# Merge and first feed-forward group in written order, with loads and casts ahead

## The chip, the cores and the metric

The kernel runs on one core of one Trainium2 chip. A core has four engines that compute and that this text names by the profile's letters too: TensorE (PE, matmuls; PEld is its weight load), VectorE (DVE), ScalarE (ACT) and GpSimd (POOL). A fifth, SyncE (SP), issues nearly all transfers between the chip's main memory (HBM) and the core's working memory (SBUF); ScalarE issues a few. Matmul results land in eight accumulation banks (PSUM). Each engine works through its own list of instructions in order, and waits at an instruction until the semaphores that it needs are up. The metric is the device time of one execution in microseconds; lower is better.

## The reference

One layer of a transformer-like block over 2048 latent tokens and 256 context tokens of width 1024, all in float32:

```python
mod = silu(c) @ w_mod + b_mod                 # sh1, sc1, g1, sh2, sc2, g2
h = modulate(x, norm1_g, sh1, sc1)
k, v, q, u, vg, ga, gb = split(h @ w_in)      # one projection
attn = attention(rope(q), [ctx keys, keys], [ctx values, values])
gm = gelu(u) * (gm_ws @ rmsnorm(gelu(vg)) + gm_bs)
y = sigmoid(ga) * (attn @ w_br_attn) + sigmoid(gb) * (gm @ w_br_gm)
x1 = x + g1 * (y @ w_out)                     # the "merge"
h2 = modulate(x1, norm2_g, sh2, sc2)
out = x1 + g2 * (relu(h2 @ w_ff1) ** 2 @ w_ff2)   # the feed-forward part
```

## The kernel before

Every float32 operand is split into a high part (a cast, on ScalarE) and the remainder (a subtraction, on VectorE or GpSimd), and a product is three matmuls: high x high, high x low, low x high (`mm3`, L183 to L185; `product`, L1502 to L1504). `split` (L150, L154) makes the two parts. The large products of the feed-forward part use a scheme of seven block products instead of eight (numbered 0 to 6), whose operands are sums and differences of blocks.

The stages, in order: input projection and gMLP (to about 730 us), attention (to 1436), the merge, and then for each of two blocks of 1024 tokens the first products (`ff1`) and the second products (`ff2`).

*The merge* goes over 4 blocks b of 512 tokens. For each, 8 branch steps m compute 128 columns of the merged rows y: 12 matmuls with the gMLP inputs and 12 with the attention inputs, each followed by a product with a gate on VectorE (L1268); the two are added (L1271) and y is split. Then the output projection: for four groups tt of 128 tokens and two halves n, 24 matmuls over the 8 parts of y, a product with the gate g1 (L1313), the residual addition (L1314), a store of x1 and a sum of squares on ScalarE (L1320). Around this, other work is woven in as Python generators that are advanced step by step: `load_w_out` (the output weights, in block 0), `br_inputs` (the inputs of the next block), `mod_part` (the modulation vectors sh2 and sc2: sixteen loads of `w_mod` each, multiplied and added up on VectorE, summed over the partitions by small matmuls) and, in the last block, `h_first` (reads x1 back, scales it (L1356), transposes it on TensorE (L189, evacuated at L1369) and makes the operands of the first products) and `w1_ops` (weights of the first products: L1450, L1451, L1456 to L1472).

*The feed-forward part.* `ff1` runs 16 groups of 256 hidden columns, each with the seven products (`ff1_group`), and stores its operands for the second half to HBM (`ao_d`). `ff2` reads them back with the second weights (`w2o_d`) in 56 chunks, casts each (L1607, L1608) and multiplies; a generator `side` runs beside it: the gate g2 (`last_gate`) and the operands of the next block (`h_ops`).

*What sets the order.* A scheduler orders the instructions of each engine by its own estimate of when they are ready, earlier-written first. `order()` at the end can forbid that: instructions in a range listed in `pins` keep the written order on every engine; those in `fixed` keep it on TensorE and VectorE alone. Before the change the attention is `fixed` and each `ff2` is pinned; the merge and `ff1` are neither. Working memory is handed out in rings: a tag with n slots (`POOLS`, L55 on) gives a new tile the slot of an old one, and its first write waits until the old one's last reader is done. Tags that matter here: `bw` (14, branch weights), `gt` (6, gates), `raw` (3) and `gx` (2) for input rows, `md` (5, modulation), `wo` (18, output weights), `xt` (3, residual rows), `f8` (2, x1 blocks and raw first weights), `b4` (12, first weights and second-product chunks). Pools are opened and closed by stage, so that the first tiles of a new pool wait for the last readers of the old ones.

Of the kernel before, what the change touches and what calls it, by code (L numbers as in the profile page):

```python
# [70 lines left out]
class Kern:  # L71
# [280 lines left out]
    def mod_part(self, alloc, names):  # L352
        nc, I = self.nc, self.I
        for what in names:
            at = 2 * D + ("g1", "sh2", "sc2", "g2").index(what) * D
            for n in range(2):
                lo, sl = at + n * TB, slice(n * TB, (n + 1) * TB)
                acc = alloc()
                for k in range(KC):
                    w = alloc()  # L360
                    nc.sync.dma_start(w, I["w_mod"][0, k * P : (k + 1) * P, lo : lo + TB])
                    s = self.silu[:, k, 0:1]
                    if k == 0:
                        nc.vector.tensor_scalar(
                            out=acc, in0=w, scalar1=s, scalar2=None, op0=ALU.mult
                        )
                    else:
                        nc.vector.scalar_tensor_tensor(
                            out=acc, in0=w, scalar=s, in1=acc, op0=ALU.mult, op1=ALU.add
                        )  # L370
                    if k % 2:
                        yield
                yield
                if what in ("g1", "g2"):
                    dst = (self.g1b if what == "g1" else self.g2b)[:, sl]
                    nc.sync.dma_start(
                        dst, I["b_mod"][:, lo : lo + TB].partition_broadcast(P)[:, 0, :]
                    )
                    ps = self.bank([TB])
                    nc.tensor.matmul(ps, self.ones, acc, start=True, stop=True)  # L380
                    nc.vector.tensor_tensor(out=dst, in0=ps, in1=dst, op=ALU.add)
                    if what == "g1":
                        nc.vector.tensor_scalar(
                            out=dst, in0=dst, scalar1=0.5, scalar2=None, op0=ALU.mult
                        )
                else:
                    ks = slice(n * HK, (n + 1) * HK)
                    bc = self.small([HK])
                    nc.sync.dma_start(
                        bc, I["b_mod"][:, lo : lo + TB].rearrange("o (k p) -> p (o k)", p=P)  # L390
                    )
                    ps = self.bank([HK])
                    for k in range(HK):
                        nc.tensor.matmul(
                            ps[:, k : k + 1], acc[:, k * P : (k + 1) * P],
                            self.ones[:, :1], start=True, stop=True,
                        )
                    dst = (self.S2 if what == "sh2" else self.G2)[:, ks]
                    nc.vector.tensor_tensor(out=dst, in0=ps, in1=bc, op=ALU.add)
                    if what == "sc2":  # L400
                        n2 = self.small([HK])
                        nc.sync.dma_start(
                            n2,
                            I["norm2_g"].rearrange("o (k p) -> p (o k)", p=P)[:, ks],
                        )
                        nc.vector.scalar_tensor_tensor(
                            out=dst, in0=dst, scalar=1.0, in1=n2, op0=ALU.add, op1=ALU.mult,
                        )
                yield

    def last_gate(self):
        nc, I = self.nc, self.I

        def fetch(n, k):
            lo = 5 * D + n * TB
            w = self.sb("f2", [TB])
            nc.sync.dma_start(w, I["w_mod"][0, k * P : (k + 1) * P, lo : lo + TB])
            return w

        steps = [(n, k) for n in range(2) for k in range(0, KC, 2)]  # L420
        nc.sync.dma_start(
            self.g2b, I["b_mod"][:, 5 * D : 6 * D].partition_broadcast(P)[:, 0, :]
        )
        ahead = [fetch(0, k) for k in range(2)]
        yield
        accs = []
        for i, (n, k0) in enumerate(steps):
            ws = ahead
            if i + 1 < len(steps):
                ahead = [fetch(steps[i + 1][0], steps[i + 1][1] + j) for j in range(2)]  # L430
            if k0 == 0:
                accs.append(self.sb("f2", [TB]))
            for k, w in zip((k0, k0 + 1), ws):
                s, acc = self.silu[:, k, 0:1], accs[n]
# [4 lines left out]
                else:  # L439
                    nc.vector.scalar_tensor_tensor(  # L440
                        out=acc, in0=w, scalar=s, in1=acc, op0=ALU.mult, op1=ALU.add
                    )
            yield
        for n in range(2):
            dst = self.g2b[:, n * TB : (n + 1) * TB]
            ps = self.bank([TB])
# [1728 lines left out]
```

## Time and profile before

| | |
|---|---|
| time, median of 3 executions (range) | 3094.04 us (3090.9 to 3099.88) |
| time of the profiled execution | 3104.55 us |
| span in its profile | 3102.5 us |
| mean granted TensorE clock | 0.983 |
| TensorE busy | 2994.0 us (97%) |
| VectorE, ScalarE, GpSimd busy | 2074.6, 1459.5, 689.0 us |
| moved by transfers | 534.32 MB |

The profile comes from one execution, recorded by the hardware. A row of a timeline gives start, duration, engine, line and operation, what is written from what (names of tiles without numbers), and in brackets how long the engine had been idle before it and which instruction of which engine released it. A row of a table by groups gives the number of instructions, their busy time and mean duration in ns, then the idle time before them. A row of a table by windows gives for each engine the busy time and in brackets the number of instructions, then the granted TensorE clock as a share of full speed, the busy share of the transfer engines and what they moved. Matmuls overlap in the array, so one row of 0.39 us may start 0.23 us after the one before.

### The profile page before, as it was taken

To read this page: it belongs to the slowest core of one execution; us is meant where nothing else is said; L and a number is where in the kernel's file an instruction comes from. 1 tells how busy PE (TensorE), PEld (TensorE's weight loads), DVE (VectorE), ACT (ScalarE), POOL (GpSimd) and SP (SyncE) were. 2 spreads that over 40 slices of the span, in tenths; PEclk is the share of its full clock that TensorE was granted. 3 is DMA by queue.
4 is the path that set the end of the run, shared out by engine and by line. 5 is a ranking of instruction groups with operands and counts; after the bars stand their busy time and mean duration, and the time that the engine had idled before them with its cause. 6 is when DMAs were issued, how large, how long until landed. Compare 5 with 4: busy or idle time off the path is not lost.

```text
span 3102.5 us, 38027 instructions
## 1 busy us (share of the span) xinstructions
PE 2994.0 (97%) x13501; PEld 2262.9 (73%) x13501; DVE 2074.6 (67%) x2990; ACT 1459.5 (47%) x2352; POOL 689.0 (22%) x506
## 2 busy tenths in 40 slices
PE   6999999979999999999989999999999999999999
PEld 4877788766555555556867878887878888878887
DVE  4767578875887667777654478775676666654555
ACT  5645765654555454554222155443454344444432
POOL 0000000001988888885134300000000000000000
PEclk9999999999999999999999999999999999999999
DMA  8676666644110000005865448887776544438554
GB/s 296 202 259 212 226 197 198 205 145 129 35 35 28 14 15 8 11 15 185 265 203 164 137 156 316 310 301 278 256 234 220 191 153 153 154 139 285 204 200 153
DMA packets 386478, 534.32 MB, mean 172 GB/s; under 512 B 32928, under 2 KB 204112, under 8 KB 386288
## 3 DMA queue, kind: packets, MB, share of 16 engines
q1 hardware_dynamic: 376512, 515.89, 49.7%
q10 hardware_dynamic: 9776, 16.01, 1.4%
q8 instruction: 106, 1.74, 0.2%
q14 instruction: 84, 0.69, 0.1%
HBM read 367.69 MB, written 164.10 MB: 171 GB/s over the span
## 4 chain that ended last, share of the span: by engine, by line
PE 83%; DMA 6%; DVE 5%; ACT 2%; issue 2%; POOL 1%; SPq 0%; ACTq 0%; DVEq 0%; POOLq 0%
PE b L1502 14%; PE b L1503 14%; PE b L1504 14%; PE b L2067 8%; PE b L2034 5%; PE b L2053 4%; PE b L183 3%; PE b L185 3%; PE b L184 3%; PE a L1502 3%; PE b L1999 3%; PE a L1503 3%; PE a L1504 3%; PE b L189 2%; DMA bw<-in_w_br_gm 1%
## 5 line engine op out<-in xcount | busy, mean ns | idle before, releaser
L2010 DVE TENSOR_REDUCE ts<-b 128x1 f32<-128x512 f32 x512 | 314.7, 681 | 141.6 <-PE b L1999 141.5
L2083 POOL TENSOR_TENSOR ac<-ac,p 128x512 f32<-128x512 f32 x216 | 301.5, 1428 | 67.7 <-ACT p L2057 67.0
L1608 DVE TENSOR_TENSOR b<-b,b 128x1024 fp32r<-128x1024 f32 x168 | 198.6, 1221 | 145.0 <-ACT b L1607 144.6
L1607 ACT CAST b<-b 128x1024 fp32r<-128x1024 f32 x168 | 168.7, 1051 | 240.0 <-PE b L1503 222.0
L2057 ACT ACTIVATE p<-b 128x512 f32<-128x512 f32 x384 | 199.8, 616 | 166.5 <-PE b L2053 156.6
L1502 PE MATMUL b<-b,b 128*128 128x512 f32 x672 | 263.9, 393 | 8.6 <-ACT b L1607 7.9
L1503 PE MATMUL b<-b,b 128*128 128x512 f32 x672 | 263.1, 391 | 2.4 <-DVE b L1608 2.4
L1504 PE MATMUL b<-b,b 128*128 128x512 f32 x672 | 262.6, 391 | 0.0
L2083 POOL TENSOR_TENSOR ac<-ac,t 128x512 f32<-128x512 f32 x152 | 217.6, 1457 | 0.0
L2034 PE MATMUL b<-h,h 128*128 128x512 f32 x576 | 200.9, 419 | 0.9 <-DVE ts L2010 0.4
L2053 PE MATMUL b<-h,h 128*128 128x512 f32 x576 | 180.3, 394 | 0.0
L2067 PE MATMUL b<-p,h 128*64 128x512 f32 x768 | 175.3, 598 | 0.0
L1503 PE MATMUL b<-hb,b 128*128 128x512 f32 x448 | 174.6, 390 | 0.0
L1956 POOL MEMSET t<- 128x512 f32 x16 | 8.4, 525 | 701.9 <-DMA tb_d<-t 679.8
L1502 PE MATMUL b<-hb,b 128*128 128x512 f32 x416 | 162.0, 389 | 0.0
L1504 PE MATMUL b<-hb,b 128*128 128x512 f32 x416 | 161.7, 389 | 0.0
L1512 DVE TENSOR_TENSOR f<-f,b 128x512 f32<-128x512 f32 x160 | 109.2, 682 | 77.7 <-issue 46.1
L1502 PEld LDWEIGHTS b<-b,b 128*128 128x128 f32 x672 | 126.9, 189 | 36.6 <-ACT b L1607 9.2
L2034 PEld LDWEIGHTS b<-h,h 128*128 128x128 f32 x576 | 106.7, 190 | 58.4 <-DVE ts L2010 19.4
L1503 PEld LDWEIGHTS b<-b,b 128*128 128x128 f32 x672 | 126.8, 189 | 30.0 <-DVE b L1608 3.7
L1504 PEld LDWEIGHTS b<-b,b 128*128 128x128 f32 x672 | 126.8, 189 | 26.5
L1502 PE MATMUL a<-f,h 128*128 128x384 f32 (+1 forms) x320 | 118.7, 376 | 12.8 <-ACT f L647 6.3
(409 smaller groups left out, 7435.0 us busy)
## 6 DMA issues: line engine op xcount, KB each, us to landing
ao_d<-f SPq DMA_DIRECT2D x224, 256.0 KB
f<-in_w_ff SPq DMA_DIRECT2D x48, 1024.0 KB
b<-ao_d SPq DMA_DIRECT2D x84, 512.0 KB
b<-w2o_d SPq DMA_DIRECT2D x84, 512.0 KB
w2o_d<-f SPq DMA_DIRECT2D x112, 256.0 KB
f<-in_w_in SPq DMA_DIRECT2D x44, 512.0 KB
f<-x_d SPq DMA_DIRECT2D x64, 256.0 KB
hb<-ao_d SPq DMA_DIRECT2D x56, 256.0 KB
```

Source lines behind the costliest of these rows:

```text
L1502: mm(ps, wh, hh, start=start and k == 0, stop=False, skip_group_check=True)
L1503: mm(ps, wh, hl, start=False, stop=False, skip_group_check=True)
L1504: mm(ps, wl, hh, start=False, stop=k == len(w) - 1, skip_group_check=True)
L1512: nc.vector.tensor_tensor(out=out, in0=in0, in1=in1, op=op)
L1607: nc.scalar.copy(h, f32(l))
L1608: nc.vector.tensor_tensor(out=l, in0=f32(l), in1=f32(h), op=ALU.subtract)
L2010: nc.vector.tensor_reduce(out=self.mx[:, t, h, c : c + 1], in_=ps[h], axis=AX.X, op=ALU.max)
L2034: self.nc.tensor.matmul(self.pts[j][h], k.KA[c][self.kv][:, ks], self.qa[h], start=True, stop=False, skip_group_check=True,)
L2053: self.nc.tensor.matmul(s, k.KB[c][self.kv][:, ks], self.qb[h], start=False, stop=True, skip_group_check=True,)
L2057: self.nc.scalar.activation(pt[h], s, AF.Exp)
L2067: nc.tensor.matmul(self.o[h * HD : (h + 1) * HD, :], k.V[c][:, i, self.kv * HD : (self.kv + 1) * HD], pt[h], start=j == 0, stop=j == NKT - 1,)
L2083: nc.gpsimd.tensor_tensor(out=self.acc[e][:, h], in0=old[:, h], in1=pt[h], op=ALU.add)
```

## The change

- The whole merge, from its first load to the last residual store, is a pinned range: every engine keeps the written order.
- Branch step n issues the loads of raw weights and gates of step n+2 and casts the weights of n+1. Before, it loaded and cast those of n+2 together. Remainders of weights go to GpSimd from the third step on (before: in blocks 1 to 3); the remainder of y goes from GpSimd to VectorE.
- `load_w_out`, `br_inputs`, the residual rows and `mod_part` fetch one step ahead. The broadcast row sums of `br_inputs` use the tag `gx`. The store of x1 and its square come after the next group's first products. `next(side)` and `next(mod)` come before the two VectorE operations of the projection instead of after them.
- `mod_part` loads its bias at the start of a part instead of at its end, and does g2 as well, in place of `last_gate`.
- `h_first` scales a block one step before it is transposed, and makes the sums one step after. The merge advances it by 1 + 7 steps, and by 2 more after the pinned range. The casts of the very first weights take a slot of `f8` in place of two of `b4`.
- In the very first group of `ff1`, product 5 comes after product 1.
- The first block's second products load three chunks ahead instead of two, and the first two chunks are loaded before the last group of first products.

The core of the diff:

```diff
     def load_w_out(self):
         ...
-        for k in range(KC):
+        ahead = fetch(0)
+        yield
+        for k in range(KC):
+            st = ahead
+            if k + 1 < KC:
+                ahead = fetch(k + 1)
             h, l = self.sb("wo", [D], F32R), self.sb("wo", [D], F32R)
             self.split(st, h, l, lo_eng="dve")
     def merge(self, first, start, last, ops, w1):
         ...
+        begin = self.here()
         steps = [(b, m) for b in range(NB) for m in range(KC)]
         ...
+        def load(n, tag="gt"):
+            raws[n] = self.br_raw(steps[n][1])
+            gts[n] = self.gate_in(*steps[n], tag)
+
+        def cast(n, lo_eng):
+            ws[n] = self.br_weights(raws.pop(n), lo_eng)
...
+        load(0, "gx")
+        load(1)
+        cast(0, "dve")
+        next(w_out)
         for b in range(NB):
             y = []
             for m in range(KC):
-                fetch("pool" if b else "dve")
-                ws, gt = q.pop(0)
+                n = b * KC + m
+                if n + 2 < len(steps):
+                    load(n + 2)
+                if n + 1 < len(steps):
+                    cast(n + 1, "pool" if n > 1 else "dve")
+                w, gt = ws.pop(n), gts.pop(n)
...
-                self.split(gt["a"], yh, yl)
+                self.split(gt["a"], yh, yl, lo_eng="dve")
...
+            next(side)
+            xt, done = x_row(b, 0), None
             for tt in range(TT):
-                xt = self.sb("xt", [D])
-                nc.sync.dma_start(xt, self.x_block(b)[tok, :])
+                after = x_row(b, tt + 1) if tt + 1 < TT else None
...
                     outer(n, range(head if tt == 0 else 0, KC))
+                    if n == 0 and done:
+                        stored(*done)
+                        done = None
+                    if b + 1 < NB or (tt, n) < (TT - 1, 1):
+                        next(side, None)
+                    next(mod, None)
                     part = self.sb("jk", [512])
                     nc.vector.tensor_tensor(out=part, in0=ps, in1=self.g1b[:, cs], op=ALU.mult)
                     nc.vector.tensor_tensor(out=xt[:, cs], in0=xt[:, cs], in1=part, op=ALU.add)
-                    next(side, None)
-                    next(mod, None)
-                nc.sync.dma_start(self.x1_d[b][tok, :], xt)
...
+                done, xt = (b, tt, xt), after
+            stored(*done)
...
+        self.pins.append(range(begin, self.here()))
+        for _ in range(2):
+            next(side)
     def h_first(self, ops, w1):
+        x, raw = self.x1_load(0, 0), None
+        yield
+        for kk in range(HK):
+            self.x1_scaled(x, r)
+            if kk:
+                sums(kk - 1, raw)
+            yield
+            raw = self.x1_turned(x, kk)
+            if kk + 1 < HK:
+                x = self.x1_load(0, kk + 1)
+            else:
+                next(w1)
+            yield
+        sums(HK - 1, raw)
+        next(w1)
+        yield
     def w1_ops(self, g, out, first=False):
-        hr, lr = self.sb("b4", [KC, P], F32R), self.sb("b4", [KC, P], F32R)
+        if g == 0 and first:
+            both = self.sb("f8", [2, KC, P], F32R)
+            hr, lr = both[:, 0], both[:, 1]
...
     def ff1_group(self, blk, g, w, h):
-        self.product(pb, w[5], h[5], True)
-        u2 = self.sb("f2", [TB])
-        tt(u2, u3, pb, add)
-        yield
+        if g or blk:
+            u2 = fifth()
+            yield
         self.product(pa, w[1], h[1], False)
...
+        if not g and not blk:
+            u2 = fifth()
+            yield
     def ff1(self, blk, h, extra, w=None, late=()):
-                self.ready = [self.ff2_cast(self.ff2_load(blk, 0, 0))]
+                raws = [self.ff2_load(blk, 0, c) for c in range(2)]
+                self.ready = [self.ff2_cast(raws.pop(0))], raws
     def ff2(self, blk, side):
-        ahead = 4 if blk else 2
+        ahead = 4 if blk else 3
...
-        ready = self.ready
-        raws = [load(n) for n in range(1, ahead)]
+        ready, raws = self.ready
+        raws += [load(n) for n in range(2, ahead)]
     def ffn(self, h, w, w1, late):
-        next(late)
-        next(late)
+        next(late)
...
-        side = chain(self.last_gate(), self.h_ops(1, h))
+        side = chain(
+            self.mod_part(lambda: self.sb("f2", [TB]), ("g2",), True), self.h_ops(1, h)
+        )
```

252 lines of the change are left out of this document (123 added, 129 removed).

## The prediction

> **What bounds the kernel now.** I read the page first, the busy time of the engines.
>
> ```profile
> span 3102.5 us, 38027 instructions
> PE 2994.0 (97%) x13501; PEld 2262.9 (73%) x13501; DVE 2074.6 (67%) x2990; ACT 1459.5 (47%) x2352; POOL 689.0 (22%) x506
> ```
>
> TensorE is busy 97% of the span, so an edit that removes no matmuls can win only where TensorE idles, or runs at a lowered clock after idling. The changed code runs from 1436.7 us (first branch product of the merge) to about 2520 us (end of the first block's second products). The waits of TensorE told me where to cut that stretch; this view gives busy time and counts of each window.
>
> ```profile
> core 0: us, PE busy (x) PEld busy (x) DVE busy (x) ACT busy (x) POOL busy (x), PEclk, DMA share, GB/s
> 1436.70:1553.00 116.30, 116.22 (x497) 93.06 (x498) 80.56 (x111) 37.58 (x60) 23.36 (x16) 0.99 0.84 269
> 1553.00:1605.00 52.00, 42.37 (x162) 31.47 (x161) 34.58 (x38) 13.68 (x24) 26.35 (x19) 0.90 0.67 216
> 1678.00:1705.00 27.00, 23.13 (x88) 17.89 (x87) 12.94 (x18) 8.60 (x15) 8.01 (x7) 0.87 0.61 199
> 1705.00:1776.00 71.00, 71.00 (x314) 57.94 (x313) 27.63 (x39) 13.94 (x25) 22.99 (x17) 1.00 0.39 126
> 1828.00:1846.00 18.00, 12.59 (x34) 8.83 (x35) 16.42 (x23) 12.11 (x19) 0.00 (x0) 0.72 0.45 149
> 1846.00:2150.00 304.00, 304.00 (x1334) 249.95 (x1333) 236.98 (x325) 144.60 (x212) 0.00 (x0) 1.00 0.83 293
> 2150.00:2170.00 20.00, 12.38 (x41) 9.32 (x40) 8.03 (x8) 6.18 (x6) 0.00 (x0) 0.74 0.99 346
> ```
>
> The counts tell more than the busy time. Undisturbed, the merge does 314 matmuls in 71 us: 4.42 per us, 0.226 us each. Against that rate the second window lacks 52 x 4.42 - 162 = 68 matmuls (15.3 us), the third 31 (7.1 us), the one at 1828 lacks 46 (10.3 us), the one at 2150 lacks 47 (10.7 us). These figures hold idle time and lowered clock together. So 43 us, 1.4%, is there to be won; the rows of 1.00 clock are full.
>
> What makes the first hole is seen in the timelines of ScalarE, VectorE and TensorE (start, duration, instruction, idle time before it and its releaser).
>
> ```profile
> 1583.01 0.62 ACT L150 CAST bw<-bw 128x512 fp32r<-128x512 f32 x1 [4.73 <-DMA bw<-in_w_br_gm]
> 1585.34 0.62 ACT L150 CAST bw<-bw 128x512 fp32r<-128x512 f32 x1 [1.71 <-POOL bw L154]
> 1585.87 1.13 ACT L150 CAST in<-raw 128x512 fp32r<-128x512 f32 x2
> 1586.90 0.62 ACT L150 CAST y<-gt 128x512 fp32r<-128x512 f32 x1
> ...
> 1583.50 0.69 DVE L1271 TENSOR_TENSOR gt<-gt,gt 128x512 f32<-128x512 f32 x1
> ...
> 1587.58 0.80 PE L183 MATMUL b<-wo,y 128*128 128x512 f32 x1 [5.30 <-ACT y L150]
> ```
>
> The merged rows y that the output projection needs are added up by 1584.2 (L1271), but ScalarE casts them only at 1586.90: they stand in its queue behind weights for later steps, which wait for their load and for GpSimd. TensorE idles 5.30 us for sums that were ready after 2 of them.
>
> The hole at 2150 is another kind:
>
> ```profile
> 2149.34 0.32 SPq L1560 DMA_DIRECT2D ao_d<-f  x1
> 2150.09 0.37 SPq L1595 DMA_DIRECT2D b<-ao_d  x1
> ...
> 2155.43 1.04 ACT L1607 CAST b<-b 128x1024 fp32r<-128x1024 f32 x1 [6.84 <-DMA b<-ao_d]
> ...
> 2157.86 0.80 PE L1502 MATMUL b<-b,b 128*128 128x512 f32 x1 [7.15 <-ACT b L1607]
> ```
>
> Chunk 1 of the second products is loaded only after the group's last stores, takes 5.3 us to its cast, and TensorE has nothing for 7.15 us.
>
> **The change, part by part.** *Merge in program order.* No matmul, cast or gate load goes away; their order does. Within step n, ScalarE now casts the weights of n+1 and then y of n. The load of those weights was issued two steps ahead; residual rows, `w_out`, the next block's inputs and the modulation weights are issued one step ahead. A step is 24 matmuls, 5.4 us, so two steps are 10.9 us, against the 5.3 us that the load above took at the fullest DMA (share 0.99). Newly queued: SyncE, in order, holds the gate loads of n+2 until y of n-1 is split, which frees their slots, and the raw weights of n+3 stand behind them; they are still issued about 10 us before their cast. The groups of the two middle blocks (1553 to 1776 us) give the loop that is left:
>
> ```profile
> L154 POOL TENSOR_TENSOR bw<-bw,bw 128x512 fp32r<-128x512 f32 x38 | 50.7, 1348 | 131.3 <-ACT bw L150 131.3
> L154 POOL TENSOR_TENSOR y<-gt,y 128x512 fp32r<-128x512 f32 x22 | 32.0, 1457 | 9.9 <-ACT y L150 9.9
> ...
> L150 ACT CAST bw<-bw 128x512 fp32r<-128x512 f32 x38 | 22.4, 619 | 86.6 <-DMA bw<-in_w_br_gm 68.8 <-POOL bw L154 10.8 <-PE b L185 6.2
> ...
> L1268 DVE SCALAR_TENSOR_TENSOR gt<-gt,b 128x512 f32<-128x512 f32 x43 | 29.0, 683 | 46.8 <-PE b L185 46.8
> L1271 DVE TENSOR_TENSOR gt<-gt,gt 128x512 f32<-128x512 f32 x21 | 19.4, 923 | 0.6
> L154 DVE TENSOR_TENSOR in<-raw,in 128x512 fp32r<-128x512 f32 x16 | 15.2, 953 | 19.9 <-ACT in L150 19.9
> ```
>
> From the end of step n: gate product 0.68, addition 0.92, y on ScalarE 0.62, the cast of the weights of n+2 0.62, GpSimd's remainder 1.35: 4.2 us; in block 0 the cast of a `w_out` row comes between (128x1024, 1.04 like L1607 above): 5.2 us. That remainder is first read by the third matmul of step n+2, 5.4 + 0.5 = 5.9 us later. So the loop closes with 1.7 us to spare, in block 0 with 0.7. GpSimd's load falls from 2 x 1.35 + 1.46 = 4.2 us a step to 2.7; VectorE's rises by the 0.95 of y's remainder to 2 x 0.68 + 0.92 + 0.95 = 3.2 us, in block 0 by a wider `w_out` remainder more. Both stay below 5.4. In the output projection VectorE has, per 24 matmuls, one input row (a product 0.69 as the single L1271 above, a remainder 0.95), two modulation rows (taken as 0.92 each) and two additions (0.69 each): 4.9 us. That is tight too, but it holds TensorE up only if the block's last input is late, and this one has 12 matmuls of gMLP products (2.7 us) as cover; with the cover gone I would expect 2 us at each of three block starts. I take both holes as gone, -22.4 us, and put 2.5 us back for these tight places, nearer to none than to the bound, as the loop has slack in every block (bounds 0 and +9, which is about one us in each step of block 0).
>
> The subtraction that moves from GpSimd to VectorE now runs beside GpSimd's remainders. The Trainium skill, "SBUF — State Buffer", in its part on the port that both engines share, says that a VectorE instruction with two SBUF inputs is shut out for the whole of a GpSimd instruction that reads SBUF. The groups agree in direction: 0.92 and 0.95 with two SBUF inputs, 0.68 with one in PSUM. At worst, by that rule, y would come 1.35 us later, which uses up most of the slack.
>
> *End of the merge, first group.* The hole at 1828, ScalarE and then TensorE:
>
> ```profile
> 1829.37 1.06 ACT L1320 ACTIVATE jk<-xt 128x1024 bf16<-128x1024 f32 x1 [5.59 <-DVE xt L1314]
> 1830.33 0.19 ACT L1320 ACTIVATION_READ_ACCUMULATOR jk<-xt 128x1 f32 x1
> 1830.42 1.03 ACT L1450 CAST b<-f 128x1024 fp32r<-128x1024 f32 x1
> 1831.36 0.77 ACT L1369 ACTIVATE f<-b,S,G 128x512 f32<-128x512 f32 x1
> ...
> 1831.50 0.80 PE L1502 MATMUL b<-in,b 128*128 128x512 f32 x1 [3.62 <-ACT b L1450]
> ...
> 1839.85 0.50 PE L1504 MATMUL b<-in,b 128*128 128x512 f32 x1 [1.68 <-DVE b L1466]
> ```
>
> The last 16 transposes move from before the last projection to after it, and product 5, which waited 1.68 us, comes after product 1 and so gets 12 matmuls, 2.7 us, more. Against that, the new buffer for the first weights (L1450) is free only when these transposes are done, and the four activations out of them (0.77 each), the square (1.06) and one cast (0.62) can stand ahead of it on ScalarE: 4.8 us, of which some 0.3 to 1.3 us lie before the transposes' end. That puts the first product 3.5 to 4.5 us after the transposes, against 3.62 us of wait before. VectorE was busy 16.42 of 18 us and has the same work. I take 0 (bounds -5, half the hole, and +6).
>
> *Second products.* Chunk 1 is now loaded before the last group of first products, so TensorE goes on at 2150.7 for 24 matmuls, to 2156.1. Chunk 2 is then the first that is loaded at 2150.1; it lands as chunk 1 did, and its first matmul can start at 2157.9: 1.8 us of idle, 1 us more for its remainder on VectorE, and an estimated 2 us of lowered clock after that. 10.7 becomes 4.8, so -5.9 us (bounds -10.7 and 0, the latter if the extra 1 MB finds no free slot in the last group). In the steady state the twelve slots are as full before as after. On the clock, the window at 1678, whose granted mean is 0.87, lost 27 x 0.13 = 3.5 us in that way. The Trainium skill, "TensorE: Matmul & The Clock Gate", Part 1, says that the clock halves after an idle window of about 3.4 us; by that rule a wait of 2.8 us would cost no clock and the sum would be 2 us lower.
>
> *The rest.* Gate g2 takes 13 instead of 10 of 56 slots, bias loads come earlier, the attention's last input loads one step ahead. None of them ends a wait of TensorE in the rows above: 0. If the cover of the g2 slots went, its first use in step 15 of 56 would be late by at most those 3 slots.
>
> Sum: -22.4 + 2.5 + 0 - 5.9 = -25.8 us. The profiled execution took 3104.55 us, 10.5 above the median of 3094.04; taken off the median, 3068.
>
> **Rivals.** *A, slower: the loop of a branch step is longer than a step.* VectorE's split of y and GpSimd's remainders delay each other, and ScalarE, in program order, casts the next weights behind y. From 1.7 us of delay on TensorE waits in every step; at 2.6 us it loses 0.9 us in each of 29 steps and the gain is gone; at 3.2 us it loses 1.5 x 29 = 43 us: 3068 + 43 = 3111. For it: 953 against 683 ns. Against: GpSimd's load falls by a third. *B: the holes stay by half*, because the loads are late and not the casts' order: SyncE too is now held behind gates and stores that wait. +11, and chunk 1 finds no slot, +6: 3085. For it: 269 GB/s in block 0, whose loads stay. Against: 126 GB/s in the undisturbed window. *C: the end of the merge gets worse by 10*: VectorE's sums of the last quarter, six of 0.69, come ahead of the first weights' remainder: 3078. *D: chunk 2 comes in time too, and half the hole at 1828 goes*: -4.8 - 5: 3058.
>
> **How the numbers follow.** Forecast 0.53, D 0.12, C 0.10, B 0.10, A 0.15. A measurement of this kernel can tell about 0.3%, 9 us, from no change. Forecast, C and D are faster (0.75), B counts as same (0.10), A is slower (0.15). The predicted time is the forecast's, 3068. The range goes from 3052 (D, the 2.5 us not paid, and a little clock kept) to 3095 (B with the tight places at their bound); A lies outside.
>
> **What would show it.** Right: between 1437 us and the last projection no window that lacks more than a few matmuls, no wait of L183 for ScalarE's y above 1 us, the last projection ending some 20 us earlier, and the wait for L1607 down from 7.15 to under 3. Wrong: TensorE waits for `bw` in step after step (A), waits for y at block starts (B), or for more than 6 us at the first group (C).

## The result, and the profile after

The changed kernel took 3070.71 us in the median (3068.4 to 3072.42), the kernel before, run beside it, 3096.32 us (3090.9 to 3099.88): ratio 0.992, 95% interval 0.9906 to 0.9933. Measured again beside the last experiments it was 3073.59 against 3101.74 us, ratio 0.9909 (0.9895 to 0.9923). So it is faster by 25.6 us, where 25.8 had been predicted, and the 3070.71 us stand against 3068.

That the total fits says little yet. The time of one execution differs from the next by up to about 10 us in the part ahead of the merge, which the change hardly touches (the first branch product starts anywhere between 1432.0 and 1442.9 us in the traces of this study; 1437.5 and 1441.5 in two executions of after). The stages behind it repeat better, so the accounts below are made by three stages, each read from first and last starts. The per-line views of before and of after give them (number of instructions, shortest, median and longest duration in ns, first and last start):

```profile
L183 PE MATMUL b<-in,bw x256: 392/396/628, 1436.7 to 1776.4; 128*128 128x512 f32 x128
...
L185 PE MATMUL b<-wo,y x256: 388/389/795, 1485.1 to 1827.5; 128*128 128x512 f32 x128
...
L1502 PE MATMUL b<-b,b x672: 387/389/796, 2145.1 to 3089.7; 128*128 128x512 f32 x168
```

```profile
L183 PE MATMUL b<-in,bw x256: 392/395/632, 1437.5 to 1752.9; 128*128 128x512 f32 x128
...
L185 PE MATMUL b<-wo,y x256: 389/389/400, 1486.3 to 1803.1; 128*128 128x512 f32 x128
...
L1545 PE MATMUL b<-b,b x680: 387/389/799, 2124.9 to 3057.9; 128*128 128x512 f32 x170
```

The merge runs from the first branch product to the last matmul of the output projection: 1827.5 - 1436.7 = 390.8 us before, 1803.1 - 1437.5 = 365.6 after. The first group's stage runs from there to the first matmul of the second products: 317.6 and 321.8. The rest runs to the end of the span (3102.5 and 3070.6): 957.4 and 945.7. The differences are -25.2, +4.2 and -11.7 us. Of the first two, 1.9 us are only moved: the last 16 transposes now stand behind the merge. The same table for all kernels of this study, with the measured ratio to the kernel before:

| kernel | merge | to second products | second products to end | ratio (95%) |
|---|---|---|---|---|
| before | 390.8 | 317.6 | 957.4 | 1 |
| after | 365.6 | 321.8 | 945.7 | 0.9920 (0.9906 to 0.9933) |
| after, run again | 365.7 | 321.8 | 946.0 | 0.9909 (0.9895 to 0.9923) |
| e1_free | 365.2 | 321.9 | 945.8 | 0.9920 (0.9898 to 0.9942) |
| e2_pin_only | 378.7 | 319.6 | 957.1 | 0.9969 (0.9957 to 0.9981) |
| e3_y_pool | 367.2 | 323.3 | 948.0 | 0.9929 (0.9912 to 0.9945) |
| e4_one_chunk | 365.6 | 322.2 | 957.9 | 0.9946 (0.9927 to 0.9965) |
| e5_load1 | 385.3 | 325.1 | 947.9 | 0.9978 (0.9966 to 0.9989) |
| e6_p5_first | 366.2 | 324.0 | 946.3 | 0.9911 (0.9894 to 0.9928) |
| e7_load_only | 368.4 | 317.6 | 955.6 | 0.9929 (0.9915 to 0.9942) |
| e8_chunks_only | 387.3 | 318.3 | 943.7 | 0.9956 (0.9943 to 0.9969) |
| e9_two_edits | 370.2 | 317.6 | 944.3 | 0.9904 (0.9889 to 0.9919) |
| v1_turn_early | 367.4 | 319.4 | 947.5 | 0.9903 (0.9887 to 0.9920) |
| v2_in_place | 364.3 | 324.8 | 945.7 | 0.9907 (0.9890 to 0.9923) |

Where the text below gives a ratio, its interval stands here. Two executions of the same kernel (after, and after run again) agree within 0.3 us in each stage. A stage with holes repeats less well: the merge of e8_chunks_only, in which TensorE, VectorE, ScalarE and GpSimd run the same sequence of instructions as in before, took 387.3 us and before's own 390.8. So less than 3.5 us is not read as an effect, and a gain counted against before's merge is uncertain by that much. The merges of e7_load_only and v2_in_place hold a gain of 1.6 us by a chance of the clock, told in the last section.

The page of after, then the windows of its TensorE in which something was or is to be seen (length, busy time and count, granted clock, share of the transfer engines, GB/s):

```profile
span 3070.6 us, 38002 instructions
PE 2981.3 (97%) x13501; PEld 2256.5 (73%) x13501; DVE 2070.4 (67%) x3006; ACT 1457.8 (47%) x2350; POOL 656.7 (21%) x488
```

```profile
1580.00:1600.00 20.00, 20.00 (x89) 1.00 0.63 218
...
1680.00:1700.00 20.00, 20.00 (x94) 1.00 0.74 227
...
1800.00:1820.00 20.00, 12.96 (x53) 0.83 0.34 118
1820.00:1840.00 20.00, 18.86 (x75) 0.91 0.68 224
...
2120.00:2140.00 20.00, 19.05 (x84) 1.00 0.68 238
...
2760.00:2780.00 20.00, 19.06 (x83) 1.00 0.97 351
```

A full window of 20 us holds 87 to 94 matmuls. Both holes of the merge are gone, and so is the one at the start of the second products (2120). The hole at the end of the merge is still there, and larger: 128 instructions in 40 us, 16 of them short transposes. The waits of TensorE from 1430 to 1860 us say the same (what it waited for, us in total, times, longest):

```profile
PE b L1545 <- ACT f L1493: 3.4, 1, 3.4
PE b L1545 <- ACT in L1367: 3.1, 1, 3.1
PE b L183 <- ACT bw L150: 1.8, 1, 1.8
PE b L1546 <- DVE in L1368: 0.8, 1, 0.8
PE b L1547 <- DVE f L1494: 0.8, 1, 0.8
```

There is no wait for y at all, and the only one for `bw` is that for the very first weights, 1.75 us in before and after alike. Between the first branch product and the end of the merge TensorE idled 13.5 us in before and ran 20.5 us at a granted clock of 0.5; in after it does not idle, and runs 3.4 us at that clock.

The loop of a branch step as it now runs, from the timelines of ScalarE, GpSimd and VectorE:

```profile
1565.51 0.62 ACT L150 CAST y<-gt 128x512 fp32r<-128x512 f32 x1 [3.94 <-DVE gt L1296]
1566.04 1.14 ACT L150 CAST bw<-bw 128x512 fp32r<-128x512 f32 x2
...
1566.73 2.55 POOL L154 TENSOR_TENSOR bw<-bw,bw 128x512 fp32r<-128x512 f32 x2 [3.05 <-ACT bw L150]
...
1564.79 0.69 DVE L1296 TENSOR_TENSOR gt<-gt,gt 128x512 f32<-128x512 f32 x1
1566.17 0.69 DVE L154 TENSOR_TENSOR y<-gt,y 128x512 fp32r<-128x512 f32 x1 [0.69 <-ACT y L150]
```

ScalarE waits for one thing only, the sum of the gated products. The weights' casts follow y at once and wait for nothing. From the end of a sum to the start of y's cast it takes 0.04 us on average, against 1.2 us, and up to 7.8, in before.

### The profile page after: what moved, and what is told of

Its sections match the earlier page's. It is cut to its first block, busy times and chain, and to the rows that moved or that the text cites. A ratio compares the mean times of both kernels' runs of the same rounds, so it can differ in the third digit from the quotient of the medians.

```text
span 3070.6 us, 38002 instructions
## 1 busy us (share of the span) xinstructions
PE 2981.3 (97%) x13501; PEld 2256.5 (73%) x13501; DVE 2070.4 (67%) x3006; ACT 1457.8 (47%) x2350; POOL 656.7 (21%) x488
## 4 chain that ended last, share of the span: by engine, by line
PE 84%; DVE 6%; DMA 5%; ACT 2%; issue 2%; SPq 0%; ACTq 0%; DVEq 0%
PE b L1546 13%; PE b L1545 13%; PE b L1547 13%; PE b L2121 8%; PE b L2088 5%; PE b L2107 4%; PE b L183 4%; PE b L185 4%; PE b L184 4%; PE b L2053 3%; PE a L1545 3%; PE a L1546 3%; PE a L1547 3%; PE b L189 2%; DMA f<-in_w_in 1%
## 5 line engine op out<-in xcount | busy, mean ns | idle before, releaser
L2137 POOL TENSOR_TENSOR ac<-ac,p 128x512 f32<-128x512 f32 x216 | 300.3, 1423 | 69.4 <-ACT p L2111 68.8
L1546 PE MATMUL b<-b,b 128*128 128x512 f32 x680 | 266.3, 392 | 5.6 <-DVE b L1661 5.6
L1545 PE MATMUL b<-b,b 128*128 128x512 f32 x680 | 267.1, 393 | 3.3 <-ACT b L1728 1.4
L1547 PE MATMUL b<-b,b 128*128 128x512 f32 x680 | 265.3, 390 | 0.0
L1558 ACT ACTIVATE f<-f 128x512 f32<-128x512 f32 x96 | 60.5, 630 | 148.8 <-DVE f L1555 148.8
```

What stands on the lines that cost most here:

```text
L1545: mm(ps, wh, hh, start=start and k == 0, stop=False, skip_group_check=True)
L1546: mm(ps, wh, hl, start=False, stop=False, skip_group_check=True)
L1547: mm(ps, wl, hh, start=False, stop=k == len(w) - 1, skip_group_check=True)
L2137: nc.gpsimd.tensor_tensor(out=self.acc[e][:, h], in0=old[:, h], in1=pt[h], op=ALU.add)
```

## The experiments

The question was which part of the change closes the holes of the merge. The prediction's theory, called O here, was the order of ScalarE's queue. Its rival, L, was lateness: the casts were queued so close behind their loads that ScalarE waited for the transfers.

**e1_free**: the changed kernel, its merge no longer pinned.

```diff
-        self.pins.append(range(begin, self.here()))
```

> The changed kernel, but the merge is no pinned range any more: the scheduler orders it again. Loads two steps ahead and casts one step ahead stay as they are written. Theory O (order: TensorE idled because ScalarE had casts of later weights ahead of y in its queue): holes of 15 to 22 us come back in the merge, 3086 to 3093 us. Theory L (lateness: the loads came too late, and the loads ahead are what helped): at most 5 us are lost, 3071 to 3076 us.

3073.89 us, ratio 0.9920, all three stages within 0.5 us of after. The written order is not needed: with loads and casts where the change has put them, the scheduler keeps every hole closed too. As a cause that stands alone, O falls.

**e2_pin_only**: the reverse, the kernel before with its merge pinned in its own written order, and nothing else.

```diff
         self.open("late", side="right")
+        begin = self.here()
 ...
+                self.pins.append(range(begin, self.here()))
```

(The second line stands at the end of the branch steps of the last block.)

> The kernel before, with nothing changed but that the merge, up to the last block's output projection, is a pinned range. Loads and casts of a step still stand together, two steps ahead. Theory O: most of the 22 us of the merge are gained, 3074 to 3082 us. Theory L: a cast stands right behind its own load and ScalarE now waits for it in order, so no gain, 3090 us or more.

3089.64 us, ratio 0.9969, the merge shorter by 12.1 us: half of what the change brings there. The waits of TensorE from 1430 to 1860 us (the five largest):

```profile
PE b L183 <- ACT bw L150: 3.7, 2, 2.0
PE b L1504 <- ACT b L1452: 3.6, 1, 3.6
PE b L183 <- ACT in L150: 2.5, 2, 1.5
PE b L1506 <- DVE b L1468: 1.7, 1, 1.7
PE b L184 <- DVE wo L154: 1.1, 2, 0.7
```

The waits for y, 8.7 us in the kernel before, are gone, as O has it. Before's row of the same view:

```profile
PE b L183 <- ACT y L150: 8.7, 4, 5.3
```

In their place stand small ones for weights, inputs and `wo`, which the written order puts too close behind their loads. So order does close the large holes of before, but opens others.

**e5_load1**: the changed kernel, pinned, with the raw weights loaded one step ahead instead of two, and cast right behind the load.

```diff
-        load(1)
 ...
-                if n + 2 < len(steps):
-                    load(n + 2)
+                if n + 1 < len(steps):
+                    load(n + 1)
```

> The changed kernel with raw weights and gates loaded one step ahead in the written order instead of two; casts stay one step ahead, so a cast stands right behind its own load. Theory O: SyncE runs ahead of the other engines as far as the slots allow, so the time to a cast is hardly shorter: 0 to +4 us, 3071 to 3075. Theory L: each cast waits some 3 us for its load, the slack of the loop (1.7 us) is gone, 1 to 2 us lost in each of 29 steps: 3100 us or more.

3093.24 us, ratio 0.9978: the merge takes 385.3 us, so 19.7 of its 25.2 us are lost, with every other part of the change in place. TensorE waits for weights again, five times, the longest at 1477.91:

```profile
PE b L183 <- ACT bw L150: 11.7, 5, 4.9
```

In the steady steps the loads of this kernel still run ahead of their casts, by 7.9 us between an issue and the first cast behind it. The holes come in four places, in block 0 and at the starts of the other blocks, where that distance falls to 3.3 to 4.1 us. At the first of them SyncE, which works in the written order too, was held up by a store that waited 9.7 us for VectorE. In after a load is held up there as well (3.0 us to its cast), but it is that of one step later, and TensorE does not wait. So the second step of lead is cover for such places, as far as these rows show.

**e7_load_only**: the distance alone. In the kernel before, only the cast is moved one step back from its load. The scheduler orders the queues, y's remainder stays on GpSimd, and the other loads stay as they were.

```diff
-        def fetch(lo_eng="pool"):
-            s = next(it, None)
-            if s is not None:
-                q.append((self.br_weights(self.br_raw(s[1]), lo_eng), self.gate_in(*s)))
+        def load(n, tag="gt"):
+            raws[n] = self.br_raw(steps[n][1])
+            gts[n] = self.gate_in(*steps[n], tag)
+
+        def cast(n, lo_eng):
+            q[n] = self.br_weights(raws.pop(n), lo_eng)
 ...
-                fetch("pool" if b else "dve")
-                ws, gt = q.pop(0)
+                n = b * KC + m
+                if n + 2 < len(steps):
+                    load(n + 2)
+                if n + 1 < len(steps):
+                    cast(n + 1, "pool" if b else "dve")
+                ws, gt = q.pop(n), gts.pop(n)
```

> The kernel before, with one edit in the merge: the cast of the branch weights moves one step later (weights of n+1 are cast in step n, raw weights of n+2 are loaded there), so the cast stands a whole step behind its load. Nothing else of the change, the planner orders the queues, y's remainder stays on GpSimd. Theory L (the distance between load and cast is the lever, whoever orders): all of the merge's gain, 20 to 25 us less than before, ratio 0.992 to 0.9935, no wait of TensorE for y above 1 us. Theory I (it takes the new distance together with the loads of inputs, residual rows and w_out one step ahead): 5 to 15 us less, ratio 0.995 to 0.9985, with waits for inputs or w_out left at block starts.

3080.43 us, ratio 0.9929. The merge takes 368.4 us: 22.4 of the 25.2 us, from one edit. Counted with care it is 17 to 22: the same edit took 370.2 us in e9_two_edits below, and before's merge repeats between 387.3 and 390.8. The waits of TensorE for y shrink to 0.5 us and those for y's remainder to 1.2:

```profile
PE b L185 <- POOL y L154: 1.2, 2, 0.6
...
PE b L183 <- ACT y L150: 0.5, 2, 0.4
```

One row of the table by groups helps to compare these kernels: what ScalarE's weight casts waited for between 1553 and 1776 us (before has 86.6 us, 68.8 of them for the transfer: that row stands in the prediction). Here are e1_free, e2_pin_only, e5_load1, e7_load_only and after, in this order:

```profile
L150 ACT CAST bw<-bw 128x512 fp32r<-128x512 f32 x35 | 21.8, 622 | 56.2 <-PE b L184 33.8 <-POOL bw L154 21.8 <-DMA bw<-in_w_br_gm 0.6
```

```profile
L150 ACT CAST bw<-bw 128x512 fp32r<-128x512 f32 x38 | 21.7, 618 | 29.7 <-DMA bw<-in_w_br_gm 25.1 <-PE b L184 2.8 <-POOL bw L154 1.8
```

```profile
L150 ACT CAST bw<-bw 128x512 fp32r<-128x512 f32 x40 | 22.7, 616 | 12.4 <-DMA bw<-in_w_br_gm 10.4 <-POOL bw L154 2.0
```

```profile
L150 ACT CAST bw<-bw 128x512 fp32r<-128x512 f32 x37 | 23.0, 623 | 65.2 <-POOL bw L154 34.5 <-PE b L184 27.4 <-DMA bw<-in_w_br_gm 3.2
```

```profile
L150 ACT CAST bw<-bw 128x512 fp32r<-128x512 f32 x38 | 21.6, 615 | 0.0
```

In e7_load_only ScalarE's casts still wait 65.2 us, nearly all of it for other things (GpSimd, free slots), and the merge is nearly as short as after's; e1_free shows the same. The waits for the transfer have gone, from 68.8 to 3.2 us, and with them the holes. What hurts is not that a cast waits, but that y stands behind it: y's cast starts 1.2 us after its sum on average in before, and 0.15 us in e7_load_only. The sum of the waits alone does not rank the kernels, and the window leaves out block 0. From 1430 to 1830 us the casts wait for the transfer 88.7 us in before, 44.0 in e2_pin_only and 26.0 in e5_load1, though the merge of e5_load1 is the longer of the last two.

The distance is bound up with the ring of 14 `bw` slots. In the kernel before, step n holds the cast weights of n and n+1 (8 slots) and takes 2 raw and 4 cast ones for n+2: all 14, so the raw load waits for slots and its cast follows at once. In the timelines of before, the second raw load of a step is issued at 1567.12 and cast at 1570.25, 3.1 us later. With the cast a step later, the ring holds 4 + 4 cast and 2 + 2 raw slots, 12 of 14; in after, the load issued at 1562.20 is that of the cast at 1571.64, 9.4 us later. Taken over the steps between 1553 and 1776 us the median of this distance is 3.3 us in before, 5.3 in e7_load_only and 9.4 in after: 2 us more were enough for nearly all of the gain.

```profile
1567.12 0.38 SPq L1216 DMA_DIRECT2D bw<-in_w_br_gm  x1
...
1570.25 1.14 ACT L150 CAST bw<-bw 128x512 fp32r<-128x512 f32 x2 [5.22 <-DMA bw<-in_w_br_gm]
```

```profile
1562.20 0.46 SPq L1221 DMA_DIRECT2D bw<-in_w_br_gm  x1
...
1571.64 1.14 ACT L150 CAST bw<-bw 128x512 fp32r<-128x512 f32 x2
```

What the issue of these loads waited for between 1553 and 1776 us agrees with this. It is GpSimd's remainder, the last reader of the raw slots, in before and then in e7_load_only (us in total, times, longest):

```profile
SPq L1216 <- POOL bw L154: 41.0, 25, 4.6
```

```profile
SPq L1216 <- POOL bw L154: 7.5, 15, 1.0
```

A larger ring with the order of before was not tried.

**e3_y_pool**: the changed kernel with y's remainder back on GpSimd.

```diff
-                self.split(gt["a"], yh, yl, lo_eng="dve")
+                self.split(gt["a"], yh, yl)
```

> The changed kernel with the remainder of y on GpSimd as before. By the loop worked out in the prediction GpSimd then has 4.2 of 5.4 us a step, still below the step: 0 to +3 us, 3071 to 3074. Rival G (GpSimd's load was part of the holes): waits for the bw remainders return in every step, 0.7 us in some 20 steps, +10 or more.

3077.97 us, ratio 0.9929, the merge longer by 1.6 us. All three stages are longer by about 2 us, two of which the edit does not touch, so no effect can be told from chance. The 10 us or more of rival G do not show in the merge.

**e4_one_chunk** and **e8_chunks_only** take the second products. The first is the changed kernel with the loads of before, the second the kernel before with the new loads alone. The diff is that of e8_chunks_only:

```diff
-                self.ready = [self.ff2_cast(self.ff2_load(blk, 0, 0))]
+                raws = [self.ff2_load(blk, 0, c) for c in range(2)]
+                self.ready = [self.ff2_cast(raws.pop(0))], raws
 ...
-        ahead = 4 if blk else 2
+        ahead = 4 if blk else 3
 ...
-            return self.ff2_load(blk, *steps[n], bool(blk) and n % 2 == 1)
+            return self.ff2_load(blk, *steps[n], blk and n > 2 and n % 2)
 ...
-        ready = self.ready
-        raws = [load(n) for n in range(1, ahead)]
+        ready, raws = self.ready
+        raws += [load(n) for n in range(2, ahead)]
```

> The changed kernel with the loads of the first block's second products as before: one chunk before the last group, two ahead. If the hole at the start of the second products was the late chunk 1, a wait of about 7 us and 3.5 us of lowered clock come back: +10.7, 3081 us. Rival: the transfers are the limit there either way, at most +4.

> The kernel before, with the second products' chunks loaded three ahead and nothing else. As the prediction had it (one hole, at 2150): 5 to 7 us less than before. As the trace of the run that put the old loads back has it (the hole comes at the start of the second products of both blocks, 47 and 34 matmuls short): 10 to 16 us less, ratio 0.995 to 0.9968, and both waits for the first cast below 1 us.

e4_one_chunk took 3084.33 us, ratio 0.9946; its last stage is 12.2 us longer than after's. e8_chunks_only took 3087.72 us, ratio 0.9956; its last stage is 13.7 us shorter than before's. Both sizes are twice what the prediction had for this edit. The waits of TensorE in e4_one_chunk say why:

```profile
2136.35 0.80 PE L1545 MATMUL b<-b,b 128*128 128x512 f32 x1 [6.02 <-ACT b L1659]
...
2772.98 0.79 PE L1545 MATMUL b<-b,b 128*128 128x512 f32 x1 [6.03 <-ACT b L1659]
```

The hole comes at the start of the second products of each block, and there are two blocks. The kernel before had the second one too, in a window that the prediction does not show:

```profile
2780.00:2800.00 20.00, 15.15 (x54) 0.83 0.77 274
```

At the prediction's full rate 88 matmuls fit into these 20 us: 34 are missing, 7.8 us. In e8_chunks_only the same two places, 2149.03 and 2779.39, show 0.94 us of idle each at a granted clock of 1.00.

**e6_p5_first**: the changed kernel with product 5 ahead of product 1 in the very first group too, as before.

```diff
-        if g or blk:
-            u2 = fifth()
-            yield
+        u2 = fifth()
+        yield
 ...
-        if not g and not blk:
-            u2 = fifth()
-            yield
```

> The changed kernel with product 5 of the very first group ahead of product 1 again. If the later place of product 5 hides the wait for its weights and inputs, a wait of 3 to 6 us more appears there: +2 to +6 us. Rival: VectorE's work sets the end of the hole whatever the order: 0.

3074.19 us, ratio 0.9911. The stage of the first group is 2.2 us longer than after's, which is within the spread, and the time is the same: the move of product 5 brings 2 us at most. Product 5 waits 3.52 us here for the cast of its operand and 3.12 in after, so the later place hardly shortens that wait.

**The end of the merge.** After's largest hole is left there. Its waits, and what holds ScalarE:

```profile
1808.64 0.79 PE L1545 MATMUL b<-in,f 128*128 128x512 f32 x1 [3.38 <-ACT f L1493]
...
1820.30 0.51 PE L1545 MATMUL b<-in,b 128*128 128x512 f32 x1 [3.12 <-ACT in L1367]
```

```profile
1811.87 0.78 ACT L1398 ACTIVATE f<-b,S,G 128x512 f32<-128x512 f32 x1 [3.29 <-DVE hb L1368]
```

The fourth evacuation of the last transposes waits 3.29 us for a slot (tag `f2`). The sums that product 5 needs come behind it, and TensorE waits 3.12 us for their cast. That the evacuation is what makes them late is read from the order of the rows. Two versions meant to be better than after try this. **v2_in_place** writes one of the sums in place, which takes one `f2` slot per quarter less. **v1_turn_early** adds to that: the last transposes, the first operand's cast and the first weights' casts come ahead of the last projection, and the fourth evacuation is left for later.

```diff
-            s1, s2 = (self.sb("f2", [TB]) for _ in range(2))
+            s1, s2 = self.sb("f2", [TB]), raw[0, 0]
 ...
-            tt(out=s2, in0=s1, in1=raw[0, 0], op=sub)
-            ops[5][kk] = self.halves(s2, 5)
             tt(out=raw[1, 0], in0=raw[0, 0], in1=raw[1, 0], op=sub)
+            tt(out=s2, in0=s1, in1=s2, op=sub)
+            ops[5][kk] = self.halves(s2, 5)
```

```diff
+                    if b + 1 == NB and (tt, n) == (TT - 1, 0):
+                        next(side)
 ...
-        for _ in range(2):
-            next(side)
+        next(side)
```

> The changed kernel with one sum of the first block's operands (s2) written over its source, so that a quarter takes 5 slots of the f2 ring instead of 6. Before it 4 + 4 + 5 + 6 = 19 tiles are wanted of 16 slots when the last quarter is summed. Theory S (the second wait at the first group, 3.1 us, is a wait for f2 slots): it shrinks, -2 to -5 us. Rival D (VectorE's queue is full there whatever the slots): 0.

> As v2_in_place, and the last quarter's transposes, the cast of its first operand and the casts of the first weights stand before the last output projection (the fourth transposed block stays in its accumulation bank until a slot is free). If the first wait of the first group (3.4 us for the first weights' cast) comes from these standing behind the transposes, it goes, with the lowered clock after it: -4 to -9 us against the changed kernel, 3062 to 3067. Rival: the work only moves the wait to product 5, 0 to -2.

Neither helps. In v2_in_place the fourth evacuation still waits 3.29 us; product 5 then waits only 0.18 us, but product 1, which comes before it, waits 2.94 us for its own last operand. Merge and first group together take 687.4 us in after, 689.1 in v2_in_place and 686.8 in v1_turn_early, and the ratios, 0.9907 and 0.9903, are after's own (0.9909 and 0.9920). In v1_turn_early the two waits became 3.0 and 2.4 us: other casts of the same first group are late at the same place. What bounds this place stays open.

**e9_two_edits**: the edits of e7_load_only and e8_chunks_only together on the kernel before, beside after itself run again.

> The two edits together, on the kernel before, and nothing else of the change. If the two are independent and carry the gain: the sum of the two, 30 us or more less than before, at or below the changed kernel (ratio 0.988 to 0.992). If other parts of the change are needed: above 0.994.

> The changed kernel as it is, beside the two edits on the same chip: 0.9920 again, within 0.0015.

3071.42 us, ratio 0.9904 (0.9889 to 0.9919), against 3073.59 us and 0.9909 for after. That is 30.3 us less than before; the two edits alone brought 21.3 and 14.0, so their sum of 35 is met within the intervals only. The three stages of e9_two_edits add up to 1632.1 us, those of after to 1633.1. Some 25 lines carry the whole gain; pinning, the other loads ahead, y's remainder on VectorE, the new order of `h_first` and the move of product 5 change nothing that can be measured in sum. By stages they take 4.6 us off the merge (370.2 to 365.6, 1.9 of it the moved transposes) and give 4.2 back at its end, 1.9 of it those transposes.

## Why the prediction was right, and where it was not

The time, 3068 forecast and 3070.71 measured, and the forecast's own case held. Its terms did not: -19.9, 0 and -5.9 us were forecast, -25.2, +4.2 and -11.7 measured. They add up to -32.7 us between the two profiles, 7 more than the difference of the medians; the profiled execution of before lay 8.2 us above the median of the executions beside the result. Its merge began at 1436.7, not late among these traces, so a part of that excess must lie in its own three stages, and the three differences are too large by some us in sum; which of them, one trace of before cannot tell.

- *Merge, the holes.* Where they were and that both would go was right, and so was the size: -22.4 forecast, -23.3 measured without the moved transposes. The signs to look for came too: no window short of matmuls, no wait for y, the last projection 24 us earlier.
- *Merge, the cause.* This step failed in part. The prediction read that y's casts stood "in its queue behind weights for later steps, which wait for their load and for GpSimd". That names both the order and the late load, but the cure is set out as "Merge in program order", and the two are not priced apart. The runs put the distance between load and cast first: alone it brings 22.4 us (e7_load_only), program order alone 12.1 (e2_pin_only), everything but the second step of lead 5.5 (e5_load1), everything but the order all of it (e1_free). Each of the numbers against before is uncertain by some 3 us. The wait for GpSimd was no part of the holes: 34.5 us of it are left in e7_load_only. Rival B had named late loads, but as a reason why holes would stay. The change had moved those loads, and B did not come.
- *Merge, the 2.5 us put back.* They were not paid. The prediction used 923 and 953 ns for VectorE's additions and remainders. In after, between the same times, these instructions take 692 and 689 ns, and y's own remainder 692. Rival A, a loop longer than a step, was further off than thought.
- *End of the merge.* Forecast 0 between -5 and +6, measured +4.2, or +2.3 without the moved transposes. That is small, but it comes back: the stage takes 317.6 us in before, e7_load_only and e9_two_edits, and 321.8 to 322.2 in after (twice), e1_free and e4_one_chunk. The wait of the first product came as forecast (3.4 us behind the transposes). The step that failed is product 5, which was given 2.7 us more time and waits 3.12 instead of 1.68 us: its operand comes behind an evacuation that waits for a slot, though taking one slot less (v2_in_place) only moved the wait to product 1. Rival C, 10 us, did not come.
- *Second products.* The term of -5.9 us was mis-sized, by two errors. The edit acts on both blocks and one hole was counted: 10.7 us at 2150, but also 7.8 at 2780. And chunk 2 comes in time, which only rival D had: TensorE waits 0.95 us instead of 1.8 and 1, and the clock stays at 1.00 where 2 us had been set aside. By the counts of their windows the two holes give more than the stage: 47 matmuls short before and 4 after, then 34 and 5, which is 72 or 16.3 us, against 11.7. Of the other 4.6 us some 3.4 are the next point; the rest was not located.
- *The rest at 0* held only nearly. No new wait of TensorE behind 1860 us is longer than 1.4 us, but apart from the two holes the last stage of after idles 7.0 us and that of before 5.2, and after then loses the clock from 2227.7 to 2231.1, which costs 7 matmuls or 1.6 us. The 20 us around the largest of these waits, of after and then of before, each with 16 transposes:

```profile
2213.00:2233.00 20.00, 17.05 (x74) 0.91 0.81 270
```

```profile
2245.00:2265.00 20.00, 16.78 (x81) 1.00 0.68 221
```

The last stages of e8_chunks_only and e9_two_edits, in which the clock does not fall there, are 2.0 and 1.4 us shorter than after's.

So the total fits to 3 us partly by luck: two terms of 5 to 6 us were too small, one of 4 was missing on the other side, and the median of before lay below the profile from which the terms were read. The range has a slip of its own: rival B with the tight places at their bound is 3085 + 9 - 2.5 = 3091.5, as the 2.5 us are in the 3085 already, and not 3095. Nothing hangs on it.

## What to carry to other kernels

In a queue that runs in order, an instruction that waits for a transfer holds up everything behind it: here a cast that waited 4.73 us was followed by a cast of y that came 2.7 us late. Put a step of the loop between the issue of a load and the first instruction that waits for it (here 5.3 us in place of 3.3 were enough), and count the ring's slots to see whether that fits, before the order is fixed by hand. When a hole is found at the start of a stage, look for the same stage elsewhere in the span and count the hole as often as it comes. Account by stages between fixed instructions, not by whole times alone: after's stages repeated within 0.3 us where whole executions differed by up to 10. But take a second trace of the kernel before as well, since a stage with holes moved by 3.5 us.

## What the runs showed of the hardware

**One idle time, two clocks.** Every kernel here idles 1.75 us ahead of the first branch product. In 12 of 14 traces the clock falls after it, in e7_load_only and v2_in_place it does not. The 10 us from the first product on, of after and of v2_in_place:

```profile
1437.49:1447.49 10.00, 10.00 (x35) 0.83 0.81 280
```

```profile
1434.63:1444.63 10.00, 10.00 (x42) 1.00 0.86 280
```

In after the matmuls start 0.23 us apart at first and 0.43 us apart from 1439.27 on, 1.8 us after work had resumed. In e9_two_edits an idle time of 1.73 us at 2151.09 costs no clock either. So a lowered clock cannot be put down to one idle time by its length: here the same 1.75 us cost 7 matmuls, 1.6 us, or nothing. What does tell the two cases apart is a grid in time. The clock that each trace records changes, from 1430 us on, only at times that lie a whole number of 3.413 us apart, within 0.002 us (in after 1439.22, 1442.63, 1807.86, 1814.68 and so on). In the twelve traces with a fall it comes at the first grid point behind the idle time, 0.84 to 1.78 us after its end; in e7_load_only and v2_in_place that point lies 0.65 and 1.87 us after the end, at the other place in e9_two_edits 0.07, and the clock stays. This shows that the place of the idle time on the grid matters, not the rule by which the clock is lowered. The Trainium skill, "TensorE: Matmul & The Clock Gate", Part 1, describes a window that runs freely, which agrees with a fall that comes at different delays behind the same idle time; that about 3.4 us of idle are needed for it does not agree with these rows.

**VectorE beside GpSimd.** The means of VectorE's additions of two working-memory operands fell from 923 to 692 ns between the two kernels, for the same size and between 1553 and 1776 us. The changed order hardly runs them beside GpSimd's remainders there, as the rows of the branch step above show: an addition and a remainder at 1564.79 and 1566.17, GpSimd from 1566.73. In before's merge the additions and remainders of this kind that no instruction of GpSimd overlaps take 0.69 us each, and those that one overlaps up to 1.76; a product with one operand in an accumulation bank takes 0.69 us at most either way. That agrees with the rule of the Trainium skill, "SBUF — State Buffer", on the shared port, which the prediction had weighed as a risk of the change; here the change took most of the collisions away. They had not made the holes: in e7_load_only the same additions are slower still, and its merge is nearly as short as after's.

```profile
L1276 DVE TENSOR_TENSOR gt<-gt,gt 128x512 f32<-128x512 f32 x22 | 27.3, 1241 | 0.8
```
